# Moving the first expert pair's up-products ahead of the gate table, and GpSimd's row scaling behind the first gather

## Chip, cores and metric

The kernel runs on one NeuronCore of a Trainium2 chip. The metric is the device time of one execution in microseconds (us), lower is better; the median of the runs counts. In the program and in the profile, PE is TensorE, DVE is VectorE, ACT is ScalarE, POOL is GpSimd and SP is SyncE, whose queue issues most of the transfers.

## What is computed

One decoder layer on 512 tokens of width 1024. The front part (an RWKV-7 group beside a block-sparse attention group, an output projection and a LayerNorm) stays as it is. The change touches the passage from the first LayerNorm to the experts:

```python
h = _layer_norm(DEEPNORM_ALPHA * h + mix, ln1_g, ln1_b)
# in _hier_moe:
g_logits = tok @ w_group + b_group            # 4 groups, top-1
e_logits = tok @ w_expert + b_expert          # 8 experts in the group, top-2
gates = g_onehot[:, :, None] * within[:, None, :]
for gi in range(N_GROUPS):
    hid = silu(tok @ w1_exp[gi]) * (tok @ w3_exp[gi])
    out = out + (hid * gates[:, gi, :, None]) @ w2_exp[gi]
# afterwards
h = _layer_norm(DEEPNORM_ALPHA * h + ffn, ln2_g, ln2_b)
```

There are 32 experts. The three weight matrices of one take 3 MB in float32, so that the 32 take some 100 MB, all of which are read from HBM once.

## The kernel before

The residual rows lie in `hb` (four row blocks i of 128 tokens, worked in the order 3, 2, 1, 0), each in two halves n of 512 columns. For each block the router makes logits on TensorE, picks experts (`route`), counts places (`rank`) and writes the normalized rows to HBM (`norm1`, a transfer into `hdram`). `slots_of` makes a one-hot matrix of places and multiplies it on TensorE, which gives `tab`, the table of which token sits in which slot. `read_rows` turns it into the row indices `idi`. `gates` computes the weights of the chosen experts (on VectorE, with five small instructions for blocks 3, 2, 1 on GpSimd, lines 1081 to 1086), and `gates_of` multiplies them by the same one-hot matrices: the table of gates, which `read_gates` reads out into `GT` and `IDY`.

Experts are worked in 16 pairs p, 64 slots for each expert of a pair. `gather(p)` fetches the 128 token rows of a pair from `hdram` with an indirect transfer issued by GpSimd. Pair 0 needs no gather: `rows0` makes its rows `HT` from `hb` by products with a one-hot matrix. For later pairs `rows(p)` transposes the gathered rows on TensorE, and `gained` scales them on ScalarE and VectorE into `HT` (even p) or `HTs[1]` (odd p). Then come `ups(p)` (16 products with the weights `wa_` of the two experts, 32 entries in the trace), `hidden(p)` (silu, product, gate `GT`), `turn` (two transposes) and `second(p)` (the down-products with `wb_`, and a scatter of the results to `ydram`). Between `ups(p)` and the next pair's `ups`, TensorE runs `rows(p+1)`, `second(p-1)` and `turn`.

The weights go through 7 buffers for `wa_` (2 MB each) and 6 for `wb_` (1 MB each). The load of expert e + 7 waits for the `ups` that reads expert e; `load_pair(7, 7)` after `ups(0)` brings experts 7 and 8 in eight pieces, `load_a` after `ups(1)` brings 9 and 10.

`gains1` makes the residual ready for the second LayerNorm: `hb` times a scale row plus a bias row, both in `LNP`. Half n = 0 is GpSimd's, half n = 1 VectorE's, a multiplication (line 1007) and an addition (line 1012) each. Nothing needs the result before the last pairs add to `hb`. `LNP` lies in the area `b6`, and the new area `b6` holds `GA[1]` (the target of every second gather, cleared first at line 1281) and `HTs[1]`. So the first writes to `GA[1]` and `HTs[1]` wait for the last reader of `LNP`.

A planner fixes each engine's instruction order when the program is built: by the order in the text (priority), by what its own estimates say is ready, and by the order edges that `after(ins, first, ...)` adds without a semaphore. `mm` adds such edges on TensorE while `strict[0]` is set or `last[1]` is given. Waits between engines are semaphores that the planner places. `MODE` is a hand-written order of the routing steps, in which `g3 g2` are the calls of `gains1` for blocks 3 and 2; blocks 1 and 0 follow in `experts_first`.

Of the kernel before, what the change touches and what calls it, by code (L numbers as in the profile page):

```python
# [171 lines left out]
def v3(ap, a):  # L172
    return ap.rearrange("p (a b) -> p a b", a=a)
# [12 lines left out]
def layer(ctx: ExitStack, tc: tile.TileContext, xT, xt, wb, wad, pc, wla, al, gl, cst, cst2, cst3, abias, wout,  # L186
          lnp, lnt, wr, br, wex, out):
    nc = tc.nc
    PE, V, S, P, SP = nc.tensor, nc.vector, nc.scalar, nc.gpsimd, nc.sync
# [4 lines left out]
    B = [pps.tile([128, 512], F32, name=f"bank{i}") for i in range(8)]  # L194
# [17 lines left out]
    last = [None, None]  # L212
# [15 lines left out]
    def mm(o, l, r, start=True, stop=True):  # L228
        return inorder(PE.matmul(o, l, r, start=start, stop=stop, skip_group_check=True))  # L229
# [720 lines left out]
    def turned(i, n):  # L950

        pt = B[TB[i][n]]
        for k in range(4):
            tp(v3(pt, 4)[:, k, :], hb[:, i, 512 * n + 128 * k:512 * n + 128 * k + 128])
        S.activation(HT.f[:, 512 * n:512 * n + 512], pt, AF.Copy)
# [42 lines left out]
            else:  # L998
                S.activation(d, src, AF.Identity, bias=b, scale=g)

    def gains1(i, engines, wait=True):

        h = hb[:, i, :]
        for n in range(2):
            ns = slice(512 * n, 512 * n + 512)
            E = engines[n]
            ins = E.tensor_tensor(h[:, ns], h[:, ns], LNP.f[:, ns], op=OP.mult)  # L1007
            if E is V and wait:
                after(ins, placed[0], "order")
            if E is P and i == 0:  # L1010
                after(ins, g1, "order")
            E.tensor_tensor(h[:, ns], h[:, ns], LNP.f[:, 1024 + 512 * n:1536 + 512 * n], op=OP.add)  # L1012

# [44 lines left out]
    def gates(i, lg4, mx, oo, gg, og, gm, ww, ww8, ex4, e2, gs, part=None):  # L1058

        E = P if i else V  # L1060
        rb = rrs[i].bitcast(BF)
        late_ = lambda x: after(x, placed[0], "order")
        if part != 1:
            late_(V.tensor_tensor(v3(rb[:, 16:24], 4), og[:, :, None].to_broadcast([128, 4, 2]),
                                  cc("idc")[:, None, 2 * i:2 * i + 2].to_broadcast([128, 4, 2]), op=OP.mult))
        if part == 0:
            return
        late_(V.tensor_scalar(ex4, lg4, gm, None, op0=OP.subtract))
        S.activation(ex4, ex4, AF.Exp, accum_out=gs)
        late_(V.tensor_tensor(e2, mx[:, :, 1], mx[:, :, 0], op=OP.subtract))  # L1070
        S.activation(e2, e2, AF.Exp)
        V.reciprocal(gs, gs)
        V.tensor_scalar(ww[:, :, 0], e2, 1.0, None, op0=OP.add)
        V.reciprocal(ww[:, :, 0], ww[:, :, 0])
        V.scalar_tensor_tensor(ww[:, :, 0], ww[:, :, 0], gs, og, op0=OP.mult, op1=OP.mult)  # L1075
        V.tensor_tensor(ww[:, :, 1], ww[:, :, 0], e2, op=OP.mult)  # L1076
        V.tensor_tensor(ww8, oo, ww[:, :, :, None].to_broadcast([128, 4, 2, 8]), op=OP.mult)
        V.tensor_tensor(gg, ww8[:, :, 0, :], ww8[:, :, 1, :], op=OP.add)
        g4 = gg.rearrange("p g (q e) -> p q g e", q=4)
        rt = rb[:, 24:152].rearrange("p (q g e j) -> p q g e j", q=4, g=4, e=2)  # L1080
        E.tensor_tensor(rt[:, :, :, :, 3], oo[:, :, 1, :].rearrange("p g (q e) -> p q g e", q=4),
                        og[:, None, :, None].to_broadcast([128, 4, 4, 2]), op=OP.mult)
        for j in range(3):
            E.tensor_copy(rt[:, :, :, :, j], g4)
            if j < 2:
                E.tensor_tensor(g4, g4, rt[:, :, :, :, j], op=OP.subtract)
# [26 lines left out]
    def late_loads(es):  # L1113
        for e in es:
            load_a(e, SA)
# [3 lines left out]
    def count():  # L1119

        for j in range(4):
            mm(cnt[:, 0:32], onesb, mb[:, j, :], start=(j == 0), stop=(j == 3))
# [6 lines left out]
            "w": lambda i: router(), "W": lambda i: opb(i, range(7, 8), True), "L": picks, "R": ranks,  # L1129
            "T": lambda i: [turned(i, n) for n in range(2)],  # L1130
            "U": lambda i: opb(i, range(7, 8), True, [0]), "V": lambda i: opb(i, range(7, 8), True, [1]), "Q": lambda i: opb(i, range(4, 7), False, [0]), "P": lambda i: opb(i, range(4, 7), False, [1]),
            "S": lambda i: turned(i, 0), "X": lambda i: turned(i, 1), "c": lambda i: count(), "l": lambda i: late_loads([i]), "g": lambda i: gains1(i, (P, V), False)}
    for w in MODE.split():
        acts[w[0]](int(w[1]))
    for i in (1, 0):
# [9 lines left out]
    def gather(p):  # L1145
        return P.indirect_dma_start(out=GA[(p - 1) % 2].f, out_offset=None, in_=hdram,
                             in_offset=bass.IndirectOffsetOnAxis(ap=idi[:, p:p + 1], axis=0),
                             bounds_check=511, oob_is_err=False)

    g1 = gather(1)  # L1150
    for i in (1, 0):
        gates(i, *kept[i], part=1)
    for i in range(3, -1, -1):
        gates_of(i, rrs[i], OHt[i], ins)
    read_gates(True)
# [23 lines left out]
    def combine(p, units=range(8), sums=False):  # L1179
        end = p == 15  # L1180
        order = LO if end else [(i, n) for n in range(2) for i in range(4)]
        for u in units:
# [8 lines left out]
            else:  # L1191
                V.scalar_tensor_tensor(hb[:, i, ns], hb[:, i, ns], 1.0, pc_, op0=OP.mult, op1=OP.add,  # L1192
                                       accum_out=SUM.f[:, 2 * i + n:2 * i + n + 1] if p == 14 else None)

    def ups(p, ht, ph):

        for k in range(8):
            for e in range(2):
                mm(ph[64 * e:64 * e + 64, :], v3(ht.f, 8)[:, k, 64 * e:64 * e + 64],
                   wa_[2 * p + e][:, 512 * k:512 * k + 512], start=(k == 0), stop=(k == 7))  # L1200

    def hidden(p, ph):
        S.activation(hd.f, ph[:, 0:256], AF.Silu)  # L1203
# [67 lines left out]
    def experts_first():  # L1271


        for i in range(4):
            if f"g{i}" not in MODE:
                gains1(i, (P, V))
        after(SP.dma_start(rdram, RR.f), g1, "rows first")
        BB[6] = area("b6")
        GA.append(T(1024, BB[6]))
        HTs.append(T(1024, BB[6]))  # L1280
        P.memset(GA[1].f, 0.0)
        gather(2)
        strict[0], last[1] = True, last[0]

        def second(p):
            Y = YY[p % 2]
            for n in range(2):
                py = B[4 + n]
                down(p, n, py)
                if n:  # L1290
                    V.tensor_copy(Y.g[:, 512:1024], py)
                else:
                    S.activation(Y.g[:, 0:512], py, AF.Copy)
            P.indirect_dma_start(out=ydram, out_offset=bass.IndirectOffsetOnAxis(ap=IDY.i[:, p:p + 1], axis=0),  # L1294
                                 in_=Y.g, in_offset=None, bounds_check=1023, oob_is_err=False)
            loads_b(p)

        for p in range(15):
            ph = B[0] if p % 2 or p >= LATE_ else B[6]
            ups(p, HTs[p % 2], ph)  # L1300
            if p == 13:
                L2.append(area(f"a{SA[4]}"))
                G2 = T(2048, L2[0])
                for j in range(2):
                    SP.dma_start(G2.f[:, 1024 * j:1024 * j + 1024], lnp[2 + j:3 + j, :].to_broadcast([128, 1024]))
                P.tensor_scalar(G2.f[:, 0:1024], G2.f[:, 0:1024], -12.0 * K_ ** 5, None, op0=OP.mult)
                L2.append(G2)
            late_a = []
            if p < HP:
                load_pair(2 * p + 7, 7)  # L1310
            for e in range(2 * p + 7, min(2 * p + 9, 2 * LQ) if p >= HP else 0):
                if p < 4 or e == 2 * p + 7:
                    load_a(e, SA)
                else:
                    late_a.append(e)
            hidden(p, ph)
            if p < LATE_:
                rows(p + 1, dst=HTs[(p + 1) % 2])
                if p + 3 < 16:
                    gather(p + 3)  # L1320
                if p > 0:
                    second(p - 1)
                if p == LQ - 3:
                    load_pair(2 * LQ, 0)
                turn(B[3])
            else:
                cbs = lambda k: combine(p - 1, CBS[k]) if p > LATE_ else None
                if p == LATE_:
                    second(p - 1)
                    combining()  # L1330
                    back()
                cbs(0)
                turn(B[3])
                cbs(1)
                py = bank((4, 5))
                down(p, 0, py)
                parts(0, py)
                cbs(2)
                rows(p + 1, (0,), HTs[(p + 1) % 2])
                cbs(3)  # L1340
                rows(p + 1, (1,), HTs[(p + 1) % 2])
                if p + 3 < 16:
                    gather(p + 3)
                ot(p)
                py = bank((4, 5))
                down(p, 1, py)
                parts(1, py)
            for e in late_a:
                load_a(e, SA)
        gained_rows()  # L1350
        last_pair(SB, None)
# [253 lines left out]
```

## Time and profile before

| what | us |
|---|---|
| median of 3 runs | 764.88 |
| lowest, highest run | 761.93, 766.13 |
| the profiled execution, its own time | 767.27 |
| its span, first to last instruction | 765.2 |
| TensorE / VectorE / ScalarE / GpSimd busy in the span | 662.1 / 359.2 / 273.0 / 212.3 |

The profile is of one execution. Its times count from the first instruction. A busy share is an average over stages with different limits. The stage of this change lies between about 440 and 510 us.

### The profile page before, as it was taken

How to read it: one execution, taken by the hardware profiler on the slowest of the kernel's cores; microseconds unless marked ns; L12 is line 12 of the kernel's file. 1: busy time of each engine (PE TensorE's matmuls, PEld its weight loads, DVE VectorE, ACT ScalarE, POOL GpSimd, SP SyncE). 2: the span in 40 equal slices, each digit the busy share in tenths (PEclk: the TensorE clock that was granted, in tenths of full speed). 3: DMA queues.
4: the chain of work that ended last, by engine and by line, in shares of the span. 5: the costliest groups of instructions: out<-in, count | busy, mean ns of one | idle time of the engine just before them, and what ended most of it. 6: DMA issues, size and time to landing. Idle time of an engine off the chain costs nothing.

```text
span 765.2 us, 9700 instructions
## 1 busy us (share of the span) xinstructions
PE 662.1 (87%) x3420; PEld 412.0 (54%) x3420; DVE 359.2 (47%) x1091; ACT 273.0 (36%) x581; POOL 212.3 (28%) x302
## 2 busy tenths in 40 slices
PE   8879999889989979979999986599998989759780
PEld 2657887678668857745665775233332323213340
DVE  4287258325833574346356697522121112103975
ACT  4345443634364445445336432123131113101330
POOL 3234444534354442120000332411111111101432
PEclk9989999999999999978999995599999989988985
DMA  9611011001110110565250755299999999999503
GB/s 319 233 55 56 29 56 56 27 28 56 56 48 9 55 43 1 193 228 176 101 192 1 287 200 228 87 357 415 424 425 425 424 420 427 421 416 410 193 2 113
DMA packets 28484, 147.18 MB, mean 192 GB/s; under 512 B 5114, under 2 KB 5626, under 8 KB 20493
## 3 DMA queue, kind: packets, MB, share of 16 engines
q1 hardware_dynamic: 23676, 134.61, 45.0%
q0 software_dynamic: 4608, 11.62, 3.9%
q8 instruction: 29, 0.48, 0.2%
q10 hardware_dynamic: 144, 0.26, 0.1%
q14 instruction: 27, 0.21, 0.1%
HBM read 138.38 MB, written 15.36 MB: 201 GB/s over the span
## 4 chain that ended last, share of the span: by engine, by line
PE 28%; DMA 20%; DVE 10%; issue 1%; ACT 0%; POOL 0%; DVEq 0%; SPq 0%; ACTq 0%
PE bank L229 25%; DMA b<-in_wex 20%; PE bank L232 3%; DVE a L147 1%; DVE base L1370 1%; DVE base L1192 1%; DVE base L147 1%; DVE base L778 0%; DVE x L1075 0%; DVE base L1012 0%; DVE base L1007 0%; DVE a L1426 0%; DVE x L1076 0%; DVE x L964 0%; DVE x L1221 0%
## 5 line engine op out<-in xcount | busy, mean ns | idle before, releaser
L229 PE MATMUL bank<-a,b 128*128 128x512 f32 (+2 forms) x1112 | 301.6, 453 | 5.8 <-DMA a<-in_wex 3.4
L229 PEld LDWEIGHTS bank<-a,b 128*128 128x128 f32 (+1 forms) x1112 | 158.0, 174 | 80.0 <-issue 41.3
L229 PE MATMUL bank<-b,base 128*64 128x512 f32 (+1 forms) x412 | 93.5, 497 | 10.8 <-DMA b<-in_wex 9.0
L229 PE MATMUL bank<-a,base 128*64 128x512 f32 (+3 forms) x308 | 82.6, 616 | 11.7 <-DMA a<-in_wex 10.6
L337 POOL TENSOR_TENSOR b<-b,b 128x1024 fp32r<-128x1024 f32 x22 | 52.3, 2377 | 73.5 <-ACT b L336 64.5
L229 PEld LDWEIGHTS bank<-b,base 128*64 128x64 f32 (+1 forms) x412 | 42.5, 161 | 51.7 <-issue 37.0
L229 PE MATMUL bank<-a 128*128 128x128 f32 (+6 forms) x264 | 63.0, 371 | 8.3 <-ACT a L627 3.9
L1204 DVE SCALAR_TENSOR_TENSOR base<-bank,base 128x256 f32<-128x256 f32 x16 | 7.7, 483 | 125.9 <-ACT base L1203 125.9
L229 PEld LDWEIGHTS bank<-a,base 128*64 128x64 f32 (+2 forms) x308 | 25.7, 153 | 60.3 <-issue 41.8
L1203 ACT ACTIVATE base<-bank 128x256 f32<-128x256 f32 x16 | 6.1, 384 | 134.4 <-PE bank L229 134.4
L229 PEld LDWEIGHTS bank<-a 128*128 128x128 f32 (+2 forms) x264 | 37.7, 199 | 22.0 <-issue 6.5
L229 PE MATMUL bank<-a,a 128*128 128x128 f32 (+2 forms) x200 | 42.8, 333 | 2.1 <-POOL a L464 2.1
L232 PE MATMUL bank<-base,a 128*128 128x128 f32 x152 | 33.0, 298 | 9.5 <-ACT a L247 7.9
L229 PEld LDWEIGHTS bank<-a,a 128*128 128x128 f32 x200 | 32.9, 201 | 9.6 <-issue 4.0
L229 PE MATMUL bank<-base 128*128 128x36 f32 (+4 forms) x136 | 28.8, 352 | 9.3 <-DVE base L1040 6.0
L336 ACT ACTIVATE b<-b 128x1024 fp32r<-128x1024 f32 x25 | 26.3, 1057 | 26.3 <-PE bank L229 18.6
L232 PE MATMUL bank<-base 128*128 128x128 f32 x156 | 30.2, 293 | 5.1 <-DVE base L1204 3.8
L232 PEld LDWEIGHTS bank<-base 128*128 128x128 f32 x156 | 18.0, 143 | 28.4 <-issue 16.6
L229 PE MATMUL bank<-b,a 128*128 128x128 f32 x192 | 31.4, 276 | 0.3 <-DVE a L633 0.3
L232 PEld LDWEIGHTS bank<-base,a 128*128 128x128 f32 x152 | 19.3, 148 | 22.6 <-ACT a L247 8.9
L229 PEld LDWEIGHTS bank<-b,a 128*128 128x128 f32 x192 | 29.9, 191 | 2.7 <-DVE a L633 0.4
L1294 POOL DMA_INDIRECT ydram<-x,base x13 | 13.2, 1012 | 63.3 <-ACT base L1209 34.7
(302 smaller groups left out, 962.5 us busy)
## 6 DMA issues: line engine op xcount, KB each, us to landing
a<-in_wex SPq DMA_DIRECT2D x28, 2048.0 KB, 32.1
b<-in_wex SPq DMA_DIRECT2D x30, 1024.0 KB, 25.4
b<-in_wb SPq DMA_DIRECT2D x25, 512.0 KB, 3.4
a<-in_wex SPq DMA_DIRECT2D x16, 512.0 KB, 16.0
ydram<-base SPq DMA_DIRECT2D x1, 4096.0 KB
a<-ydram POOLq DMA_DIRECT2D x4, 1024.0 KB, 15.9
x<-in_wout SPq DMA_DIRECT2D x6, 512.0 KB, 4.6
a<-in_xT SPq DMA_DIRECT2D x8, 256.0 KB, 6.4
```

The lines of the kernel that those rows point to most:

```text
L147: ins = f(*args, **kw)
L229: return inorder(PE.matmul(o, l, r, start=start, stop=stop, skip_group_check=True))
L232: return inorder(PE.transpose(o, i, late("ident")))
L336: S.activation(hi.f, raw.f, AF.Copy)
L337: (V if 0 < k < 4 else P).tensor_tensor(lo.f, raw.f, hi.g, op=OP.subtract)
L1192: V.scalar_tensor_tensor(hb[:, i, ns], hb[:, i, ns], 1.0, pc_, op0=OP.mult, op1=OP.add, accum_out=SUM.f[:, 2 * i + n:2 * i + n + 1] if p = ...
L1203: S.activation(hd.f, ph[:, 0:256], AF.Silu)
L1204: V.scalar_tensor_tensor(hd.f, ph[:, 256:512], GT.f[:, p:p + 1], hd.f, op0=OP.mult, op1=OP.mult)
L1294: P.indirect_dma_start(out=ydram, out_offset=bass.IndirectOffsetOnAxis(ap=IDY.i[:, p:p + 1], axis=0), in_=Y.g, in_offset=None, bounds_chec ...
L1370: E.tensor_tensor(h, h, RT[i].f[:, 1024 * r + 512 * n:1024 * r + 512 * n + 512], op=OP.add)
```

## The change

`ups(0)` is moved: it is now issued right behind the last `slots_of` product and ahead of `gates_of`, with order edges on both sides, and writes bank 0. Even pairs below 13 use bank 0 and odd ones bank 6, where before it was the other way round. (Bank 6 holds the counts `cnt` until VectorE has read them.)

GpSimd's half of `gains1` is moved for blocks 3, 2 and 1: in all four blocks it now carries an order edge to `g1`, the first gather, and is called in `experts_first`. VectorE's halves stay where they were.

```diff
-    def gains1(i, engines, wait=True):
+    def gains1(i, engines, wait=True, halves=range(2)):
 ...
-        for n in range(2):
+        for n in halves:
 ...
-            if E is P and i == 0:
+            if E is P:
                 after(ins, g1, "order")
 ...
-            ... "g": lambda i: gains1(i, (P, V), False)}
+            ... "g": lambda i: gains1(i, (P, V), False, (1,))}
 ...
     g1 = gather(1)
     for i in (1, 0):
         gates(i, *kept[i], part=1)
+
+    strict[0], last[1] = True, ins
+    ins = ups(0, HT, B[0])
+    strict[0], last[1] = False, None
     for i in range(3, -1, -1):
         gates_of(i, rrs[i], OHt[i], ins)
     read_gates(True)
 ...
         for i in range(4):
-            if f"g{i}" not in MODE:
-                gains1(i, (P, V))
+            gains1(i, (P, V), True, (0,) if f"g{i}" in MODE else range(2))
 ...
         for p in range(15):
-            ph = B[0] if p % 2 or p >= LATE_ else B[6]
-            ups(p, HTs[p % 2], ph)
+            ph = B[6] if p % 2 and p < LATE_ else B[0]
+            if p:
+                ups(p, HTs[p % 2], ph)
```

`ups` itself is moved up in the text and now returns its last instruction; its body is the same.

## Rows read from the trace of the kernel before

**Rows 1.** Chain that ended last, in order of time: start, us, what.

```profile
535.92 27.01 DMA b<-in_wex
...
660.36 31.88 DMA b<-in_wex
```

**Rows 2.** Busy time by stretch: length, engines, TensorE clock, DMA share, GB/s.

```profile
480.40:488.60 8.20, 0.00 (x0) 0.00 (x0) 8.16 (x24) 1.57 (x2) 6.92 (x9) 0.50 0.14 41
489.80:498.80 9.00, 9.00 (x37) 2.74 (x36) 0.69 (x4) 0.00 (x0) 1.08 (x1) 0.79 0.61 193
...
507.30:536.00 28.70, 28.70 (x142) 10.68 (x142) 7.78 (x18) 9.09 (x20) 5.06 (x5) 1.00 0.99 399
536.00:692.00 156.00, 133.32 (x576) 45.22 (x575) 27.67 (x58) 30.16 (x67) 21.06 (x22) 0.93 1.01 422
```

**Rows 3.** Timeline of SP's queue: start, us, what it issued.

```profile
489.68 0.33 SPq L1277 DMA_DIRECT2D rdram<-x  x1
493.57 6.46 SPq L857 DMA_DIRECT2D a<-in_wex  x8
507.32 0.80 SPq L849 DMA_DIRECT2D a<-in_wex  x2
```

**Rows 4.** Timeline of TensorE; in brackets idle time before, and releaser.

```profile
488.67 0.27 PE L229 MATMUL bank<-x 128*128 128x32 bf16 x4 [8.33 <-POOL x L1084]
489.67 0.27 PE L229 MATMUL bank<-x 128*128 128x32 bf16 x4 [0.74 <-DVE x L1084]
489.87 8.94 PE L229 MATMUL bank<-a,base 128*64 128x512 f32 x32
498.74 1.54 PE L232 MATMUL bank<-base 128*128 128x128 f32 x10
500.21 7.09 PE L229 MATMUL bank<-a,b 128*64 128x512 f32 x32
...
508.25 3.65 PE L229 MATMUL bank<-b,base 128*64 128x512 f32 x16
```

**Rows 5.** Chain that ended last, in the routing: start, us, what.

```profile
445.12 1.04 DVE x L906
...
446.18 1.38 DVE x L964
...
455.73 1.24 DVE x L1075
...
457.56 0.77 DVE x L1076
...
462.42 0.16 DVE x L964
...
470.22 1.22 DVE x L1031
...
471.78 1.07 DVE x L1036
...
480.76 0.37 DVE base L997
```

**Rows 6.** Timeline of GpSimd from the third scaled block on.

```profile
470.15 1.27 POOL L1007 TENSOR_TENSOR base<-base,b 128x512 f32<-128x512 f32 x1 [5.67 <-PE bank L229]
...
480.70 1.30 POOL L1146 DMA_INDIRECT base<-hdram,base  x1 [5.50 <-DVE x L1073]
482.03 1.28 POOL L1007 TENSOR_TENSOR base<-base,b 128x512 f32<-128x512 f32 x1
...
488.56 1.00 POOL L1281 MEMSET b<- 128x1024 f32 x1
489.84 1.08 POOL L1146 DMA_INDIRECT b<-hdram,base  x1 [0.28 <-POOL b L1281]
```

**Rows 7.** Timeline of ScalarE at the first write to `HTs[1]`.

```profile
499.49 0.85 ACT L999 ACTIVATE b<-bank,base 128x128 f32<-128x128 f32 x2 [0.21 <-PE bank L232]
```

**Rows 8.** The 15 gathers (line 1146): issue to landing.

```profile
DMA to landing us min/median/max: 4.5/10.5/13.1
```

More of the change, by code (lines that the diff above doesn't have):

```diff
@@ L1131, in layer @@
             "U": lambda i: opb(i, range(7, 8), True, [0]), "V": lambda i: opb(i, range(7, 8), True, [1]), "Q": lambda i: opb(i, range(4, 7), False, [0]), "P": lambda i: opb(i, range(4, 7), False, [1]),
-            "S": lambda i: turned(i, 0), "X": lambda i: turned(i, 1), "c": lambda i: count(), "l": lambda i: late_loads([i]), "g": lambda i: gains1(i, (P, V), False)}
+            "S": lambda i: turned(i, 0), "X": lambda i: turned(i, 1), "c": lambda i: count(), "l": lambda i: late_loads([i]), "g": lambda i: gains1(i, (P, V), False, (1,))}
     for w in MODE.split():
@@ L1148, in gather, with ups @@
                              bounds_check=511, oob_is_err=False)
+    def ups(p, ht, ph):
+        for k in range(8):
+            for e in range(2):
+                ins = mm(ph[64 * e:64 * e + 64, :], v3(ht.f, 8)[:, k, 64 * e:64 * e + 64],
+                   wa_[2 * p + e][:, 512 * k:512 * k + 512], start=(k == 0), stop=(k == 7))
+        return ins
     g1 = gather(1)
@@ L1193, in combine @@
                                        accum_out=SUM.f[:, 2 * i + n:2 * i + n + 1] if p == 14 else None)
[L1195 to L1200, printed above, removed]
     def hidden(p, ph):
```

## The prediction

> **What bounds the kernel now.** I read the chain that ended last first. From 535.92 to 692.2 us it consists of five waits for expert weights, the first of 27.01 us and the last of 31.88 [rows 1]; TensorE, VectorE and GpSimd are on it only before and behind. The table of stretches says the same: from 536 to 692 the transfer engines are busy the whole time at 422 GB/s, and from 507.3 to 536 they are at 0.99 of it already [rows 2]. So the back two thirds of the expert stage are a stream of bytes, and a change at 480 us moves the end only if it moves the beginning of that stream. The next question is when the stream begins, and what starts it.
>
> The queue of SP answers it. The first loads that depend on experts being done go out at 493.57, as the first pair's products give up their buffers piece by piece, and the next 4 MB at 507.32 [rows 3], just as the second pair's products end (500.21 + 7.09 = 507.30) [rows 4]. In front of that the transfers idle: a share of 0.14 from 480.4 to 488.6, and 0.61 from 489.8 to 498.8 [rows 2]. From 507.3 on there is no gap. The quantity that counts is therefore the end of `ups(1)`: one microsecond earlier there is one microsecond earlier at the end, as long as the stream stays fed.
>
> What sets it is TensorE's timeline. It is empty for 8.33 us, until the table of gates gets its third block at 488.67 and its last at 489.67; `ups(0)` stands in the queue behind, takes 8.94, and then come the transposes of `rows(1)` at 498.74 and `ups(1)` at 500.21 [rows 4]. But the rows of pair 0 were complete at 480.76 + 0.37 = 481.1 [rows 5]: `ups(0)` waited 8.7 us for a table that it doesn't read.
>
> **First part: ups(0) in front of the table.** Nothing is added, 16 products move. It can start when its rows come, about 480 in the clock of the trace before, instead of 489.87. The clock in the stretch is 0.50 of full (1.2 GHz) [rows 2], so I take the duration that the same products had behind that idle time, 8.94, and have it end near 489. Then TensorE waits for the gates (489.7 as before, if nothing else moves). `rows(1)` could follow at about 490 instead of 498.7: up to 8.7 us. What is late next decides how much of it stays.
>
> **What is late next: area b6.** `ups(1)` reads `HTs[1]`, which may not be written before the last reader of `LNP` is done, and this is the second part's business. Before, GpSimd had one block to scale behind the first gather: the gather at 480.70, the multiplication at 482.03, its addition, five small gate instructions, and at 488.56 the clearing of `GA[1]`, which is the first write to the new area [rows 6]. After, four blocks are scaled there: three more, six instructions, at 1.28 each and 0.03 between (the step from the gather's end, 482.00, to 482.03) [rows 6], 6 x 1.31 = 7.9 us. The area comes free at 488.56 + 7.9 = 496.4 in the clock of before, whichever order GpSimd's queue has, because all of it has to be done. This takes nearly all of the first part's 8.7 us away: ScalarE's first write to `HTs[1]` was at 499.49, and `ups(1)` began 0.72 later [rows 4, 7]; the transposes themselves write PSUM and don't wait for the area. On the first part alone `ups(1)` would begin at 496.4 + 0.7 = 497.1, 3.1 earlier than before. And since TensorE has by then stood nearly idle from 489 on, I give it the duration behind idle time, 8.94, and not the 7.09 of one that follows other work [rows 4]: 506.0, against 507.3. That is 1.3 us.
>
> **Second part: the routing without GpSimd's scaling.** This is where most of the gain should come from. When GpSimd scales, VectorE's small instructions with two inputs stand still, and the chain of waits runs through them. At 470.15 GpSimd begins a multiplication; VectorE's instruction of 4 columns at 470.22 then takes 1.22, and the next such one, at 471.78, 1.07. The same happens at 445.12 and 446.18 (1.04 and 1.38) and at 455.73 and 457.56 (1.24 and 0.77), beside the blocks scaled there; the same instruction as the one of 1.38 takes 0.16 of the chain at 462.42, when GpSimd is quiet [rows 5, 6]. The six together take 6.7; at 0.16 each they would take 1.0. So up to 5.8 us of hold-ups leave the routing, and the routing ends in the first gather. The lower bound of the gain there is the last pair alone, 1.22 + 1.07 - 0.32 = 2.0: behind it nothing but VectorE and short products lead to the gather. Of the other 3.8 a part comes back as waiting for TensorE's products for the next block, which run alongside; as the chain lies on VectorE at all four, I keep more than half, 2.2. I take 2.0 + 2.2 = 4.2 us by which the gather, the slot products, `HT` and all that follows move forward.
>
> The Trainium skill has this as a rule: in GPSIMD Engine Reference, Specifications, GpSimd's SBUF interfaces are shared with VectorE, with contention for VectorE instructions that have two SBUF inputs. The trace agrees in the places where it can be seen (1.38 against 0.16 of the chain); the rule speaks for taking the scaling out of the routing and as much against having eight such instructions beside the gates, which is the slower rival below.
>
> **The sum.** End of `ups(1)`: 496.4 - 4.2 + 0.7 + 8.9 = 501.8, where it was 507.3: 5.5 us. The bounds: with the gain of the routing at 2.0, 504.0, so 3.3; with 5.8 and a clock that stays up (7.09), 498.4, so 8.9.
>
> Does the stream stay fed? The 4 MB that go out at the end of `ups(1)` last 4.19 MB / 422 GB/s = 9.9 us. TensorE gives up the next buffers after `rows(2)` and `second(0)`, 3.65 us of down-products behind 1.5 of transposes [rows 4], so with 4.7 us to spare. The loads of experts 7 and 8 begin at about 480 or, if SP has the copy of the table to `rdram` (489.68 before, which waits for the gates) [rows 3] in front of them, at about 490; they last another 9.9 and are through by 500 either way.
>
> Everything behind, from 507 to the end, moves as one piece. The rest costs nothing: VectorE's halves stay, the banks only swap (each `ups` still has another bank than the one before it; without that it would wait for `hidden`), and the later scaling is covered by the whole stream, since the residual is next read by the last pairs; without that cover its 7.9 us would count. The span 765.2 becomes 759.7, the profiled execution 767.27 becomes 761.8. The median of the runs lies 2.4 below the profiled execution; the same difference on it gives 764.9 - 5.5 = 759.4.
>
> **The rivals.** *The routing gives little back.* If the first four hold-ups were hidden beside TensorE's work, only 2.0 goes: 3.3 us, 761.6, less than the 3.8 us (0.5%) which a measurement of this kernel tells from no change. For it: products of 512 columns run on TensorE in the same stretches. Against: the chain of waits runs through VectorE there [rows 5].
>
> *The second gather is late.* It is issued behind the clearing of `GA[1]`, at 489.84 before [rows 6], after at 489.84 + 7.9 - 4.2 = 493.5. Landing takes 4.5 to 13.1, at the median 10.5 [rows 8]: 498 to 506.6, 504.0 at the median. `rows(2)` asks for it at the end of `ups(1)`, 501.8. At the median TensorE loses 2.2 us, which the 4.7 to spare cover. With the longest landing the products of pair 2 end at 506.6 + 1.5 + 3.7 + 7.1 = 518.9, and the stream, fed at 501.8 with 9.9 us and behind `second(0)` with half as much, ends at 516.7: it runs dry for 2.2, a gain of 3.3, 761.6. If the routing gives only 2.0 besides, the same sum gives a gain of 1.1, 763.8.
>
> *The gates are held behind the scaling (slower).* Between the gather and the end of the table VectorE has 14 instructions with two inputs (ten of the gates, four scalings), and GpSimd's five for the gates stand in one queue with its scalings. If each of the 14 met a scaling at 1.1, and the planner put one scaling of 1.31 in front of each of the five, the table would be later by 15.4 + 6.6 = 22 less the 2.2 that two of them pay already: 489.7 + 19.8 - 4.2 = 505.3. `rows(1)` behind it would begin 6.6 later than at 498.7, and the end moves by that: 771.5. It decides from 498.7 on, that is from 13 us of hold-ups. Against it: eight scalings can hold eight instructions, two of which are held today, so 6 x 1.1 + 6.6 = 13 is about all there is, and the point is hardly reached. By the skill's rule alone, which knows no such limit, this is the way it would go.
>
> *The stream hides it.* That the weights are the bound and the end stays, 764.9: against it speak the idle transfers before 498.8 [rows 2].
>
> **How the numbers follow.** My forecast (a gain of over 3.8 and up to 8.9): 0.61. The routing gives little: 0.16. The second gather is late: 0.12. The stream hides it: 0.04. The gates are held: 0.07. So faster 0.61, same 0.32, slower 0.07. The likeliest is 759.4. Its bounds are 764.9 - 8.9 = 756.0 and 764.9 - 3.3 = 761.6; to hold 8 in 10 the range reaches from there up to 764.8, over the late gather to the hidden gain.
>
> **What the profile after would show.** First part: `ups(0)` behind the products with 4 columns, before the products with 32, and SP's pieces for experts 7 and 8 before 490. Second part: no GpSimd multiplication of 512 columns before the first gather, L1031 and L1036 of the last block near 0.2 of the chain each, the gather at about 476.5; then eight scalings in the queue, the clearing of `GA[1]` near 492, `ups(1)` from 493 to 502, a gap in front of it on TensorE, and the first wait for weights in the chain earlier by about 5 us. I am wrong if the gather comes later than 478.8, if TensorE waits in front of `rows(2)` for over 5 us, if the last product of the gates comes after 495, or if `ups(1)` ends on time and the transfers then show gaps.

## The result and the profile after

The kernel after takes 755.87 us at the median of four runs (755.12 to 756.99), the kernel before 765.19 (761.93 to 766.13). The ratio is 0.987, with an interval of 0.983 to 0.991: 9.3 us faster, by the interval between 6.9 and 13.0. The forecast was 759.4 and 5.5, with the range down to 756.0, which the median passes by 0.13. The profiled execution of after took 756.99 with a span of 754.9.

The chain that ended last after the change, in order of time (start, us, what), answers to [rows 1, 5]:

```profile
445.79 0.08 DVE x L906
445.90 0.26 DVE x L964
...
461.52 0.12 DVE x L1031
...
462.04 0.15 DVE x L1036
...
475.75 4.66 DVE x L1075
...
490.29 0.94 POOL b L1285
...
491.50 9.04 DMA b<-hdram,base
500.59 1.09 PE bank L232 x8
...
553.69 30.05 DMA b<-in_wex
...
650.08 31.91 DMA b<-in_wex
```

In the routing the held instructions are gone: line 964 takes 0.26 where it took 1.38, lines 1031 and 1036 of the last block 0.12 and 0.15 (1.22 and 1.07 before). Behind the gather, at 475.75, a new one stands there: line 1075, 4 columns wide, takes 4.66. Behind the clearing of `GA[1]` (490.29) the chain runs through the second gather, for which TensorE waits 0.92, and not through `ups(1)`. And it still ends in waits for expert weights, down to the last landing at 681.99.

The timeline of TensorE after, answering to [rows 4]:

```profile
471.79 2.02 PE L229 MATMUL bank<-x,base 128*128 128x128 f32 x16 [1.24 <-DVE x L920]
...
474.12 7.09 PE L229 MATMUL bank<-a,base 128*64 128x512 f32 x32
481.14 0.37 PE L229 MATMUL bank<-x 128*128 128x32 bf16 x8
489.07 0.37 PE L229 MATMUL bank<-x 128*128 128x32 bf16 x8 [7.57 <-POOL x L1084]
489.29 2.38 PE L232 MATMUL bank<-base 128*128 128x128 f32 x10
491.59 8.08 PE L229 MATMUL bank<-a,b 128*64 128x512 f32 x32
500.59 1.09 PE L232 MATMUL bank<-base,b 128*128 128x128 f32 x8 [0.92 <-DMA b<-hdram,base]
```

`ups(0)` stands in front of the gates and fills what was a wait. It took 7.09 and not 8.94. TensorE then waits 7.57 for the gates, and `ups(1)` starts at 491.59.

The timeline of GpSimd after, answering to [rows 6]; and the one row of ScalarE that answers to [rows 7]:

```profile
440.21 0.27 POOL L1081 TENSOR_TENSOR x<-base 128x32 bf16<-128x32 f32 x1
...
475.31 1.30 POOL L1146 DMA_INDIRECT base<-hdram,base  x1 [3.75 <-DVE x L1073]
476.63 2.52 POOL L1007 TENSOR_TENSOR base<-base,b 128x512 f32<-128x512 f32 x2
479.09 1.29 POOL L1012 TENSOR_TENSOR base<-base,b 128x512 f32<-128x512 f32 x1
481.25 0.65 POOL L1084 CAST x<-x 128x32 bf16<-128x32 f32 x1 [0.88 <-DVE x L1078]
481.82 1.25 POOL L1012 TENSOR_TENSOR base<-base,b 128x512 f32<-128x512 f32 x1
...
488.94 1.28 POOL L1012 TENSOR_TENSOR base<-base,b 128x512 f32<-128x512 f32 x1
490.28 0.95 POOL L1285 MEMSET b<- 128x1024 f32 x1
491.50 1.08 POOL L1146 DMA_INDIRECT b<-hdram,base  x1 [0.28 <-POOL b L1285]
```

```profile
490.47 0.46 ACT L999 ACTIVATE b<-bank,base 128x128 f32<-128x128 f32 x1 [8.80 <-PE bank L232]
```

The eight scalings lie behind the gather, and the last ends at 490.22. ScalarE's first write to `HTs[1]` follows at 490.47. So `b6` comes free just in front of it; but its row names TensorE's transposes, which stand behind the gates (489.07), as what came last. The two lie so close that this trace doesn't tell which of them sets the start of `ups(1)`; the experiments do.

Stretches of after, answering to [rows 2], with the same columns:

```profile
464.00:468.00 4.00, 4.00 (x22) 3.78 (x21) 1.70 (x10) 1.30 (x2) 0.00 (x0) 0.50 0.48 187
468.00:470.00 2.00, 1.92 (x11) 1.77 (x10) 1.55 (x18) 0.00 (x0) 0.00 (x0) 0.56 0.71 184
470.00:482.00 12.00, 9.97 (x76) 4.97 (x76) 11.09 (x37) 3.92 (x12) 6.74 (x7) 1.00 0.74 287
482.00:491.50 9.50, 2.43 (x18) 2.18 (x17) 8.59 (x16) 0.69 (x2) 9.17 (x10) 0.57 0.20 58
...
499.60:536.00 36.40, 35.48 (x174) 12.99 (x174) 8.45 (x18) 9.48 (x21) 6.06 (x6) 1.00 0.98 404
536.00:681.00 145.00, 126.06 (x546) 46.46 (x542) 26.52 (x56) 29.77 (x66) 19.22 (x19) 0.94 1.01 423
```

The granted clock from 470 to 482 is 1.00 (2.4 GHz), where it was 0.50 (1.2 GHz) throughout the corresponding passage of before. From 499.6 on the transfers are at 0.98 and then 1.01: the stream is fed. SP's queue, answering to [rows 3], and the gathers, answering to [rows 8]:

```profile
476.08 2.04 SPq L857 DMA_DIRECT2D a<-in_wex  x3
489.18 0.33 SPq L1281 DMA_DIRECT2D rdram<-x  x1
489.60 2.42 SPq L857 DMA_DIRECT2D a<-in_wex  x5
499.70 0.82 SPq L849 DMA_DIRECT2D a<-in_wex  x2
```

```profile
DMA to landing us min/median/max: 5.8/10.4/11.3
```

The pieces of experts 7 and 8 go out at 476.08; the copy to `rdram`, which waits for the gates, stands between the third and the fourth of them.

**One clock for all traces.** The part in front of the change takes several us more or less from one execution to the next. So the landmarks below are counted from GpSimd's first small gate instruction (line 1081: 439.54 before, 440.21 after), which lies ahead of everything that the change touches. Each is a start in the timelines, less that instruction's; "last gates" is the start of the last products of the gate table, and the last column is the landing of the last weights less the end of `ups(1)`.

| kernel | first gather | last gates | b6 cleared | ups(1) start | ups(1) takes | ups(1) end | rest of stream |
|---|---|---|---|---|---|---|---|
| before | 41.16 | 50.13 | 49.02 | 60.67 | 7.09 | 67.76 | 184.94 |
| before, second trace | 42.00 | 50.98 | 49.86 | 61.00 | 7.09 | 68.09 | 182.81 |
| after | 35.10 | 48.86 | 50.07 | 51.38 | 8.08 | 59.46 | 182.32 |
| first part alone | 41.81 | 50.80 | 49.69 | 53.21 | 8.91 | 62.12 | 182.33 |
| second part alone | 35.12 | 48.86 | 50.06 | 60.08 | 7.09 | 67.17 | 182.33 |
| after, gates first on GpSimd | 35.11 | 42.41 | 49.68 | 50.16 | 8.88 | 59.04 | 182.32 |
| after, copy behind the pieces | 35.11 | 48.88 | 50.08 | 51.40 | 8.26 | 59.66 | 182.30 |
| after, fillers ahead of the gates | 35.11 | 48.88 | 50.09 | 50.95 | 7.09 | 58.04 | 181.84 |
| after, scaled on VectorE | 35.10 | 41.70 | 45.95 | 46.61 | 8.78 | 55.39 | 182.48 |
| the same with fillers | 35.10 | 41.70 | 45.96 | 46.52 | 7.09 | 53.61 | 182.38 |
| second part alone, on VectorE | 36.88 | 43.46 | 47.30 | 55.00 | 7.09 | 62.09 | 182.17 |

`ups(1)` ends 8.3 us earlier than in the first trace of before, 8.6 than in the second.

### The profile page after: what moved, and what is told of

Same layout as the page of the kernel before. It is cut to its first block, busy times and chain, and to the rows that moved or that the text cites. A ratio compares the mean times of both kernels' runs of the same rounds, so it can differ in the third digit from the quotient of the medians.

```text
span 754.9 us, 9697 instructions
## 1 busy us (share of the span) xinstructions
PE 660.1 (87%) x3420; PEld 416.7 (55%) x3420; DVE 359.1 (48%) x1091; ACT 273.0 (36%) x581; POOL 211.4 (28%) x302
## 4 chain that ended last, share of the span: by engine, by line
PE 30%; DMA 18%; DVE 8%; POOL 2%; issue 1%; ACT 0%; SPq 0%; DVEq 0%; POOLq 0%; ACTq 0%
PE bank L229 26%; DMA b<-in_wex 17%; PE bank L232 4%; DVE a L147 2%; DVE base L1375 1%; DMA b<-hdram,base 1%; DVE x L1075 1%; DVE base L1204 1%; DVE base L147 1%; POOL base L1007 0%; DVE base L778 0%; POOL base L1012 0%; DVE a L1431 0%; DVE x L1226 0%; POOL x L1086 0%
## 5 line engine op out<-in xcount | busy, mean ns | idle before, releaser
L229 PE MATMUL bank<-a,b 128*128 128x512 f32 (+2 forms) x1112 | 308.7, 467 | 14.9 <-DMA a<-in_wex 12.3
L229 PEld LDWEIGHTS bank<-a,b 128*128 128x128 f32 (+1 forms) x1112 | 159.7, 177 | 94.7 <-issue 47.2
L229 PE MATMUL bank<-a,base 128*64 128x512 f32 (+3 forms) x308 | 73.5, 560 | 1.2 <-DMA a<-in_wex 0.8
L229 PEld LDWEIGHTS bank<-a,base 128*64 128x64 f32 (+2 forms) x308 | 27.3, 140 | 39.0 <-issue 27.2
```

## The experiments

**The first part alone.** The kernel before with `ups(0)` moved and the banks swapped; `gains1` as before.

```diff
+    strict[0], last[1] = True, ins
+    ins = ups(0, HT, B[0])
+    strict[0], last[1] = False, None
     for i in range(3, -1, -1):
         gates_of(i, rrs[i], OHt[i], ins)
```

> ups(0) in front of the gate table, GpSimd's scaling back in the routing. Theory A (the end of ups(1) sets the end; area b6 comes free as before, since GpSimd has one block to scale behind the gather): the gather stays near 480.7, ups(0) runs from about 480 to 488.5, last product of the gates near 489.7, ups(1) from about 491.5 and, with a clock of 0.5 at its start, 8.9 long, to 500.4, where it was 507.3: 6.9 us, time 758.3; two more if the stream adds what it added in the changed kernel. Rival, my forecast's reading (most of the gain is the routing's): a gain of 1.3, time 763.9.

760.06 us against 764.83 (ratio 0.9942, 0.9909 to 0.9975). `ups(1)` starts 7.46 earlier, takes 1.82 more and ends 5.64 earlier, not 6.9 as expected; 0.7 of what is missing is that the gates came 0.67 later in this execution. The transposes of `rows(1)` follow the gates directly. So by the traces the first part alone brings more than half (5.64 of 8.30; by the medians 4.8 of 9.3); `b6` is no hindrance to it, since GpSimd scales in the routing as before.

**The second part alone.** The kernel before with only the change of `gains1`.

```diff
-            "g": lambda i: gains1(i, (P, V), False)}
+            "g": lambda i: gains1(i, (P, V), False, (1,))}
```

> GpSimd's scaling behind the first gather, ups(0) still behind the gate table. Theory A (the scaling holds the gates there by as much as the gather came forward): the gather near 475.3, but the last product of the gates near 489, as before, ups(0) from 489.3 with 8.9, ups(1) ending near 506.7: a gain of 0.6 at most, time 764.6. Rival, my forecast (4.2 us of routing move all that follows): ups(1) ends near 503, time 761.

763.59 (1.0025, 0.9978 to 1.0071): no difference that can be measured. The gather comes 6.04 earlier, and the last gates only 1.27 earlier. The timeline of VectorE of this kernel, and under it TensorE's, show why:

```profile
474.26 4.70 DVE L1075 SCALAR_TENSOR_TENSOR x<-x 128x4 f32<-128x4 f32 x1
```

```profile
487.64 0.38 PE L229 MATMUL bank<-x 128*128 128x32 bf16 x8 [14.12 <-POOL x L1084]
487.94 9.52 PE L229 MATMUL bank<-a,base 128*64 128x512 f32 x32
```

The gates are held behind GpSimd's scalings, and `ups(0)`, which stands behind the gates here, loses nearly all that the routing had gained.

**Fillers in the routing.** The kernel before with 24 products of 256 columns that nobody reads, ahead of the last-but-one block's `rank`.

```diff
-        "... c0 l6 g3 g2 o1 o0"
+        "... c0 l6 g3 g2 o1 d24 o0"      # d24: 24 products of 256 columns
 ...
```

> The kernel before with 24 products of 256 columns that nobody reads, put where TensorE stands idle for 3.3 us in the routing (461.3 to 464.6). Theory A (the unexpected part of the routing's gain is TensorE's clock): the clock stays at 1.0, the transposes and logits of the last block (465.1 to 468.8) take about 1.9 instead of 3.7, its rows0 products 2.0 instead of 3.8, the gather comes 3 to 4 us earlier and the end as well: time 761.5 to 762.5. Rival (the clock has nothing to do with it, the hold-ups were larger than the sum of the six instructions): the gather moves by less than 0.5, time as before.

763.88 (1.0018, 0.9978 to 1.0057). The experiment missed its aim: the fillers met the lowered clock, filled the stretch to 6.92 us and held the block's `rank` back: the transposes behind it came 29.20 us after line 1081 instead of 25.59, of which 1.27 lay ahead of the fillers already. The next products were shorter (1.58 instead of 2.91 for those of `rows0` on that block), but the clock had fallen again when the last block's came, which took 3.75 as before.

**Fillers later.** The same with 13 products around the last `rank`.

```diff
-        "... c0 l6 g3 g2 o1 o0"
+        "... c0 l6 g3 g2 o1 d8 o0"       # 5 and 3 around the last rank, 5 behind the counts
```

> The kernel before with 13 products of 256 columns that nobody reads in the two idle stretches in front of the last block's rows0 products (5 and 3 around the last block's rank product, 5 behind the counts); GpSimd's scaling stays in the routing. Theory A (the clock is 0.5 there because TensorE stands idle while VectorE is held): the clock comes back before the rows0 products of the last block, they take about 2.0 instead of 3.76, and the first gather comes at 39.4 instead of 41.2, counted from GpSimd's first gate instruction of block 3. Rival (the rows0 products were shorter in the changed kernel for another reason, such as GpSimd's or VectorE's traffic): 3.4 to 3.8 as before, the gather near 41.2.

One run, 770.94, of which the part in front of line 1081 took 7.8 more than in the first trace of before. Counted from that line the gather comes at 40.45 (41.16 and 42.00 in the two traces of before) and `ups(1)` ends at 66.75. Stretches of this kernel:

```profile
479.00:482.00 3.00, 2.49 (x12) 1.91 (x12) 3.00 (x11) 0.00 (x0) 2.38 (x2) 0.50 1.03 344
482.00:489.00 7.00, 4.33 (x53) 3.63 (x53) 5.66 (x26) 3.34 (x11) 2.22 (x2) 0.93 0.37 158
```

The clock is back from 482 on, and the 16 products of `rows0` take 2.02 instead of 3.76, with GpSimd's scalings where they were. So the 1.74 us by which these products are shorter in the kernel after too are the clock's and not the scalings' own.

**The gates first.** The kernel after with GpSimd's scalings ordered behind its last instruction for the gates.

```diff
             if E is P:
-                after(ins, g1, "order")
+                after(ins, lastg[0], "order")   # GpSimd's last copy in gates
```

> The changed kernel with GpSimd's eight scalings behind its five gate instructions in its queue. Theory A (area b6, free at 490.2, and the gates, done at 489.1, bound the start of ups(1) almost equally): the last product of the gates comes near 481.5 to 483, right behind ups(0), but GpSimd is done with the scaling at 489 to 491 as before, so ups(1) starts at most 1 us earlier: time 755 to 756. Rival (the gates held behind the scaling are what sets ups(1)): ups(1) starts 4 us earlier or more, time 752.

755.75 against 764.83 (0.9915, 0.9871 to 0.996): the same as after. The gates come 6.45 earlier than in after, and `ups(1)` only 1.22, because `b6` is cleared only 0.39 earlier. So in after the gates held `ups(1)` up by less than a microsecond. It also takes 0.8 more; TensorE stood still right in front of it:

```profile
488.91 8.88 PE L229 MATMUL bank<-a,b 128*64 128x512 f32 x32 [5.72 <-ACT b L999]
```

**All scalings on VectorE.** The kernel after, GpSimd scaling nothing.

```diff
-            gains1(i, (P, V), True, (0,) if f"g{i}" in MODE else range(2))
+            gains1(i, (V, V), True, (0,) if f"g{i}" in MODE else range(2))
```

> The changed kernel with VectorE doing GpSimd's eight scalings as well. Times counted from GpSimd's first gate instruction of block 3. Theory A (area b6 is what ups(1) waits for, and its time is the sum of the scaling behind the gather): eight scalings of 1.28 leave GpSimd and eight of 0.68 join VectorE, which is held no more; the clearing of GA[1] moves from 50.1 to 47 or 48, ups(1) starts 2 to 3 us earlier and the end comes 2 to 3 us earlier than the changed kernel's: time 753 to 754. Rival (the gates set it, and VectorE now has to do both): the last product of the gates stays near 48.9 or goes later, ups(1) as before or later, time 756 to 758.

752.51 against 765.22 (0.9824, 0.9756 to 0.9892). TensorE's timeline, and GpSimd's clearing:

```profile
480.19 0.25 PE L229 MATMUL bank<-x 128*128 128x32 bf16 x4 [0.29 <-DVE x L1084]
...
483.83 0.44 PE L232 MATMUL bank<-base 128*128 128x128 f32 x2 [2.48 <-DMA a<-in_wex]
485.10 8.78 PE L229 MATMUL bank<-a,b 128*64 128x512 f32 x32 [0.82 <-ACT b L999]
```

```profile
484.44 0.95 POOL L1285 MEMSET b<- 128x1024 f32 x1 [1.46 <-DVE base L1012]
```

A scaling takes VectorE 0.68 and GpSimd 1.28, and line 1075 is held no more: it takes 0.21. (GpSimd's five small instructions for the gates still take 0.63 to 0.74 each.) `b6` is cleared 4.1 earlier and `ups(1)` starts 4.8 earlier than in after, 0.66 behind the clearing. Against the kernel with the gates first, whose gates lie only 0.71 later, `b6` is cleared 3.73 earlier and `ups(1)` starts 3.55 earlier. (The wait of 2.48 that the view puts down to a transfer ends as VectorE's `hidden`, queued behind its scalings, is done.)

**The copy behind the pieces.** The kernel after, the copy to `rdram` issued behind the eight pieces of experts 7 and 8.

```diff
-        after(SP.dma_start(rdram, RR.f), g1, "rows first")
 ...
+                pieces = load_pair(2 * p + 7, 7)
+                after(SP.dma_start(rdram, RR.f), pieces, "pieces first")
```

> The changed kernel with the copy of the table to rdram behind the eight pieces of experts 7 and 8 in SP's queue, so that all eight go out while ups(0) runs and not five of them 12 us later. Theory A (the end of ups(1) sets the end, and the pieces are through by then either way): the second gather lands in about 5 us instead of 9.0, TensorE doesn't wait 0.92 for it, the end of ups(1) and the last landing of weights stay within 0.5: time 755.5 to 756.2. Rival (the stream as a whole starts earlier): the last landing comes some 5 us earlier, time 751.

756.20 (0.9865, 0.9797 to 0.9934), `ups(1)` ends at 59.66 (59.46 in after). All eight pieces go out without a stop, the second gather lands 4.4 us after its issue instead of 9.04, and TensorE waits for it no more; yet the last weights land no earlier (241.96 behind line 1081, 241.78 in after). So neither the loads of experts 7 and 8 nor that wait cost after anything.

**Fillers ahead of the gates.** The kernel after with 30 products of 512 columns that nobody reads, where TensorE waits for the gates. (`busy(n, w)` issues n products of w columns.)

```diff
         gates_of(i, rrs[i], OHt[i], ins)
+        if i == 2:
+            busy(30, 512)
```

> The changed kernel with 30 products of 512 columns that nobody reads between the gates' second and third block, where TensorE stands idle for 7.6 us. Theory A (ups(1) is longer than 7.1 because the clock falls in that idle time): the clock stays at 1.0, the transposes of pair 1 take 1.5 or less instead of 2.4, ups(1) takes 7.1 instead of 8.1 and ends about 1 us earlier, and so does the end: time 754.8. Rival (its length comes from waiting for its rows piece by piece): ups(1) stays at 8 or more, time 755.9.

755.11 (0.9857, 0.9788 to 0.9925), within the noise of after by medians. In the trace `ups(1)` takes 7.09 instead of 8.08 and ends 1.42 earlier, the last weights land 1.9 earlier; TensorE then waits 1.47 for the second gather, which the stream covers.

**VectorE and fillers together.** The scalings on VectorE, and 14 products of 512 columns between the transposes of `rows(1)` and `turn`.

```diff
                 rows(p + 1, dst=HTs[(p + 1) % 2])
+                if p == 0:
+                    busy(14, 512)
```

> The kernel after with all four scaled blocks on VectorE, and 14 products of 512 columns that nobody reads, issued on TensorE between the transposes of rows(1) and those of turn, where TensorE waits 2.48 us in the kernel with the scalings on VectorE alone. Theory (what is left of the products' duration is the clock, as with the fillers ahead of the gates): ups(1) takes 7.1 instead of 8.78 us and ends 1.5 us earlier; the second gather then lands about 1.5 us after TensorE asks for it, which the stream covers; 751.0 us by medians. Rival (at this end the stream is bound by something else, the load of experts 7 and 8 or the second gather): ups(1) ends earlier and the end stays, 752.5.

749.69 against 766.15 (0.979, 0.9751 to 0.9828), the fastest of all. TensorE's timeline:

```profile
481.73 2.97 PE L229 MATMUL bank<-base 128*128 128x512 bf16 x13
...
485.32 7.09 PE L229 MATMUL bank<-a,b 128*64 128x512 f32 x32 [0.41 <-ACT b L999]
492.34 1.09 PE L232 MATMUL bank<-base,b 128*128 128x128 f32 x8
```

`ups(1)` starts as without them, takes 1.7 less, and the last weights land 1.9 earlier. The expected wait for the second gather didn't come: the transposes at 492.34 follow directly.

**The second part alone, on VectorE.** The second part alone, with `(V, V)` for `(P, V)`.

```diff
-        gains1(i, (P, V), True, (0,) if f"g{i}" in MODE else range(2))
+        gains1(i, (V, V), True, (0,) if f"g{i}" in MODE else range(2))
```

> The kernel before with the second part alone, but the scalings of the blocks' first halves on VectorE and none on GpSimd; ups(0) stays behind the gates. Theory (the second part alone gave only 0.6 us because the gates, which ups(0) waits for there, were held behind GpSimd's scalings): the last product of the gates comes about 8 us earlier than in the kernel before, ups(0) and ups(1) with it, less about a microsecond for VectorE's own scalings: 757.5 us. Rival (an earlier gather is of no use without the first part, whoever scales): the same as with the second part alone, 763.6.

757.27 against 766.15 (0.9879, 0.9832 to 0.9926), as the theory had it, though its gates came 6.7 earlier than before and not 8. The gather's gain reaches `ups(1)` when nothing holds the gates: 5.67 at its end, against 0.59 with the scalings on GpSimd. One thing differs that the order doesn't explain. The routing is that of the second part alone, yet the products of `rows0` took 3.76 and the gather came 1.76 later. The same passage of the second part on VectorE, and under it on GpSimd:

```profile
465.00:475.50 10.50, 7.10 (x37) 6.53 (x37) 7.58 (x58) 2.52 (x4) 1.22 (x2) 0.50 0.58 212
```

```profile
460.00:470.30 10.30, 7.09 (x37) 6.52 (x37) 7.38 (x54) 2.32 (x4) 1.21 (x2) 0.56 0.60 220
```

The same 37 products with the same busy time; in the one the clock stayed at 1.2 GHz to the end, in the other it rose just before `rows0`.

**Before once more.** The kernel before, unchanged.

> The kernel before, unchanged, for a second trace of it. Theory (the 2.6 us by which its expert stream was longer behind the end of ups(1), 184.9 against 182.3 us in every other kernel, belong to that one execution): 182.3 here. Rival (the order of the kernel before makes its stream longer): 184.9 again.

767.22, span 765.2. Its stream from the end of `ups(1)` to the last landing took 182.81, nearer to the 181.8 to 182.5 of the other kernels than to the 184.94 of the first trace. So some 2 us of that trace belong to one execution, and a comparison of its end with that of after (11.0 us, counted from line 1081) overstates the gain.

## Why the prediction was right in sign and too small

**What bounds the kernel: right.** In every kernel of the table the last weights land 181.8 to 182.8 us behind the end of `ups(1)`, the first trace of before excepted, though that end lies between 53.6 and 68.1. One microsecond there is one at the end, as forecast.

**First part: right in its mechanism.** `ups(0)` starts as its rows come, and the transposes of `rows(1)` follow the gates. Alone, these moved from 59.20 (498.74 - 439.54) to 50.91, by 8.3 of the 8.7 forecast. The duration of 8.94 given to an `ups(1)` behind an idle TensorE is what it took there, 8.91. "That is 1.3 us" for the first part failed as an attribution: the sum charged the first part with the second part's late `b6`; without that it is worth 5.6.

**Second part: the step that failed.** It is the term for the routing, 4.2 us and at the most 5.8. The gather came 6.06 earlier. The hold-ups were sized right, with some luck, as 2.2 of the 4.2 in the sum was a guess of what would be kept: they are 4.32 of the 6.06, and 4.28 in the second part on VectorE, where the products of `rows0` took 3.76 as before. The other 1.74 are these products at the higher clock, a term that the sum put at nothing, since it left TensorE's work between VectorE's instructions at its old length. The rows of TensorE in the trace of before, and a stretch of it:

```profile
473.37 0.19 PE L229 MATMUL bank<-base 128*128 128x32 bf16 x1 [1.64 <-DVE base L1040]
...
475.42 3.76 PE L229 MATMUL bank<-x,base 128*128 128x128 f32 x16 [1.24 <-DVE x L920]
```

```profile
476.00:478.00 2.00, 2.00 (x11) 2.00 (x11) 0.37 (x4) 0.43 (x2) 0.00 (x0) 0.50 0.00 0
```

TensorE's wait of 1.64 us for the held VectorE instructions, ahead of the last `rank`, closed in after; its busy stretch from 464 to 470 went on without a break, and the clock rose. The fillers around the last `rank` show that with GpSimd's scalings left in place the higher clock alone shortens these products by as much. That the change brings it each time is not shown: of eight traces with GpSimd's scalings out of the routing, seven have the 2.02 and one the 3.76. "This is where most of the gain should come from" fell too: alone the second part gives 0.6.

**Area b6: right as the next bound, 0.8 too late.** Its clearing was forecast 15.76 behind the gather (488.56 + 7.9 - 480.70) and came 14.97 behind it. The difference lies in the steps between GpSimd's instructions. The forecast gave each added one 0.03; in after many follow with none (481.25 + 0.65 = 481.90, the next at 481.82), where 0.08 lay between the same engine's instructions before (485.26 + 0.65 = 485.91):

```profile
485.26 0.65 POOL L1084 CAST x<-x 128x32 bf16<-128x32 f32 x1 [0.59 <-DVE x L1078]
485.99 0.74 POOL L1086 TENSOR_TENSOR x<-x 128x32 f32<-128x32 f32 x1
```

That `b6` bounds `ups(1)`, with the gates close in front of it, is shown by the kernel with the gates first (gates 6.45 earlier, `ups(1)` 1.22) beside the one with the scalings on VectorE (against the former, `b6` 3.73 earlier and `ups(1)` 3.55).

**The end of `ups(1)`.** It started 1.31 behind the clearing (0.7 forecast; 0.48 in the kernel with the gates first, so that the rest is the gates' share) and took 8.08 (8.9 forecast). From the forecast's 5.5: 0.1 more from hold-ups, 1.7 from the clock in `rows0`, 0.8 from `b6`, 0.6 less at the start, 0.8 from the duration, together 8.3, as measured. The fault is thus mostly a size, and the clock in `rows0` is its largest term: the range's far end took 5.8 as the most that the routing could give, and it gave 6.06. The 8.3 itself lies inside the bounds of the forecast, 3.3 to 8.9. The gain by medians, 9.3, lies a microsecond above the 8.3, inside its interval; that the median passes 756.0 by 0.13 is less than these runs can tell apart.

**The rivals.** *The gates are held behind the scaling* was no mere rival: between the gather and the last gates lie 13.76 us instead of 8.97, so 4.8 of hold-ups. That is less than the 13 from which it decides, so it cost the kernel after little (with the gates first `ups(1)` ends 0.42 earlier) and took the second part alone its whole gain. The Trainium skill says in SBUF — State Buffer, Who interferes with whom, that a VectorE instruction with two SBUF inputs contends with a GpSimd instruction that reads SBUF, and that the ports which they share are under an exclusive lock. The trace agrees: line 1075 ends at 480.41, GpSimd's third scaling at 480.38. It stood through three of them, not one; the forecast had let each scaling hold one instruction. *The second gather is late*: it landed 9.04 after its issue, and TensorE waited 0.92 for it, which the stream covered, as the kernel with the copy behind the pieces shows. *The routing gives little* and *the stream hides it* did not occur.

## What to carry to other kernels

Count an order change from landmarks of one execution, and price a moved part in the state in which the other parts leave it: here the two parts are by the traces worth 5.6 and 0.6 alone and 8.3 together, because the second part alone loses its earlier gather again while `ups(0)` waits for the gates that its scalings hold. When work leaves the chain of one engine, check whether another engine's wait closes with it, because then the products there may also run at the other clock level. And when GpSimd work with two inputs is taken out of VectorE's way in one place, ask whom it holds in the next: here VectorE itself did it in half the time, 0.68 against 1.28, and the kernel got faster by another 3.4 us (755.87 to 752.51).

## What the runs showed of the hardware

- A VectorE instruction of 4 columns with two inputs took 4.66 to 4.74 us behind the gather with three GpSimd scalings following each other without a step between them (0.21 without scalings): it did not get in between one scaling and the next. Before, where 0.08 us lay between two scalings (482.03 + 1.28 = 483.31, the next at 483.39), it ended between them, with the chain's 481.13 + 2.21 = 483.34.
- It also works the other way round: GpSimd's small instructions of the gates took 0.63 to 0.74 beside VectorE's scalings, where they take 0.25 to 0.27 alone.
- The same order of products ran at either level of TensorE's clock in different executions, 2.02 or 3.76 us for the 16 products of `rows0`. Fourteen products that nobody reads, put into a wait, saved 1.7 us of the 32 entries behind it.
